# Two PSUM banks instead of one for the accumulators of a depthwise convolution, in a two-layer decoder trunk

## The chip, the cores and the metric

The kernel runs on one core of a Trainium2 chip. A core has a matrix engine (PE; PEld is its weight load, which overlaps it), a vector engine (DVE), a scalar engine (ACT), GpSimd (POOL) and a queue that issues DMAs (SP). Each engine takes its instructions in the order in which they stand in its own program, and waits on semaphores. The metric is the device time of one execution in microseconds (us).

## The reference

Two layers of a decoder block over 256 tokens of width 1024. Each layer runs a gated feed-forward block, a mixer, a second feed-forward block and a gate with an embedding. The mixer adds attention (8 heads, a window of 128, sinks) and a convolution branch. Only the mixer is touched by the change. Its convolution branch:

```python
def _conformer_conv(a, g, w_dw, b_dw, ln_g, ln_b):
    u = a * jax.nn.sigmoid(g)
    y = lax.conv_general_dilated(
        u, w_dw[:, None, :].astype(u.dtype), window_strides=(1,),
        padding=[(CONV_WIDTH - 1, 0)],
        dimension_numbers=('NWC', 'WIO', 'NWC'),
        feature_group_count=CONV_CH) + b_dw
    return jax.nn.silu(_layer_norm(y, ln_g, ln_b))
```

There are 512 channels, and each is convolved with its own 31 taps over 256 positions. The embedding that the gate needs is `e = _rms_norm(p[i] @ w_ple[i], ple_norm[i])`; its matmuls don't depend on the mixer.

## The kernel before

All matmuls are in fp32 on 128 partitions; big weights are split into a high and a low part (ACT casts, DVE or POOL subtracts), and a product takes three matmuls. PSUM has eight banks of 128x512 fp32, dealt out by three pools: `bank` (2 buffers, projections, scores and output rows), `abank` (4 buffers) and `tbank` (2 buffers, transposes). A feed-forward stage uses its four `abank` buffers as accumulators. The mixer uses the same four for the convolution, the attention output and the embedding.

The mixer writes its parts in the order of the string `ORDER = "c0 k q c1 u s0 s1 x v0 v1 p0 o0 p1 p2 o1 p3"`:

- `c0`, `c1` (`conv_half`): the two halves of the channels. A half is 256 channels, two chunks `c` of 128. Transposed inputs stand in `uT`. The first `POOL_TAPS` taps (12 in the first half, 13 in the second) are done by ACT and POOL: ACT scales a shifted input into `pp` (two instructions, one for each chunk, into one of two `pp` buffers), POOL adds it to a sum (`yp`, named `pp` in the profile). The other taps are done by DVE, one scalar_tensor_tensor for each tap and chunk, and accumulate in PSUM (`acc`); tap by tap, chunk 0 and then chunk 1. At the end DVE adds both sums into `y`.
- `k`, `q`: keys, values and queries; `s0`, `s1` (`scores`): PE makes scores, DVE masks them and takes the maximum, ACT takes exponentials of eight pieces (`sm`), DVE makes `den` and its reciprocal, POOL spreads that (`rexp`); `v0`, `v1` (`values`): PE transposes the probabilities, DVE and ACT copy them (`pT`), PE multiplies with the values into an `abank`.
- `o0`, `o1` (`attn_out`): PE transposes `rexp`, and `o` is formed from it.
- `p0` to `p3` (`emb`, which is `part` in `ple`): one quarter of the embedding each. Two matmuls (four records in the trace) into an `abank`, then ACT squares and copies it out.

Afterwards a tail is written in a fixed order (`TAIL`): output rows of attention (`a`), the layer norm of the convolution (`s` for its statistics, from `y`; `t` for the activation, from `yn`) and output rows of the convolution (`b`).

Outside of a few stretches, the order in which instructions stand on each engine is chosen when the program is built, by a scheduler with a model of its own. The convolution's instructions are written at a lower priority (`CONV_LATER = 600`). Where a tile is written twice, the build puts in waits tile by tile: for PSUM, an instruction that writes a tile waits for the last writer of that tile even where the columns differ. A new `abank` tile waits for the last reader of the tile that had its buffer.

Of the kernel before, what the change touches and what calls it, by code (L numbers as in the profile page):

```python
# [16 lines left out]
ALU = mybir.AluOpType  # L17
# [58 lines left out]
def hybrid_trunk_kernel(  # L76
# [28 lines left out]
    V, S, GP, T = nc.vector, nc.scalar, nc.gpsimd, nc.tensor  # L105
# [10 lines left out]
    def abank():  # L116
        return ps.tile([P, 512], F32, tag="acc", name="abank", bufs=4)

    def tbank():
        return pt.tile([P, 512], F32, tag="tp", name="tbank")  # L120
# [7 lines left out]
    def small(n, name="st", dt=F32):  # L128
        return wk.tile([P, n], dt, tag=f"st{n}", name=name, bufs=16 if n == 1 else 6)
# [115 lines left out]
    def gain(l, name):  # L245
        o, n = off[name]
        return pcol[:, o + l * n:o + (l + 1) * n]
# [240 lines left out]
    def mixer_stage(l, PT, EMB):  # L488
        w = w_in[l]
        X, r, r8 = [None] * 2, [None] * 2, [None] * 2  # L490
        CI, CV = [None, None], []

        def enter(t, b):
            transposed(X, t, b, gain(l, "mix"))
            if b == 1:
                r[t] = stats(t)
                r8[t] = small(1, "r8")
                GP.tensor_scalar(out=r8[t], in0=r[t], scalar1=HD ** -0.5, scalar2=None, op0=ALU.mult)

        def proj(us, t, n, hooks=()):  # L500
            b = bank()
            mms(b[:, 0:n], x_terms(X[t], us), hooks=hooks)
            return b

        def conv_load(e):
            CI[e] = unit_pair(w, 768 + e * FC, 1280 + e * FC, KD)
            CI[e].load()

        def first(hooks):
            conv_load(0)  # L510
            CV.append(proj(CI[0], 0, 512, hooks))

        def rest(nxt):
            mixer(l, w, X, r, r8, CI, CV, proj, conv_load, PT, EMB, nxt)

        return Stage(enter, first, rest)

    def mixer(l, w, X, r, r8, CI, CV, proj, conv_load, PT, EMB, nxt):
# [3 lines left out]


        cb = gain(l, "cb")
        Y = []

        def conv_half(e):
            if e == 1:
                conv_load(1)
            tb = tbank()  # L530
            for t in range(2):
                b = CV[0] if (e, t) == (0, 0) else proj(CI[e], t, 512)
                sg = wk.tile([P, FC], F32, tag="sg", name="sig", bufs=NSG)
                S.activation(sg, b[:, FC:2 * FC], AF.Sigmoid, scale=r[t])
                uu = wk.tile([P, FC], F32, tag="h1", name="u", bufs=NH1)
                V.scalar_tensor_tensor(out=uu, in0=b[:, 0:FC], scalar=r[t], in1=sg, op0=ALU.mult, op1=ALU.mult)
                for c in range(2):
                    T.transpose(tb[:, c * 256 + t * P:c * 256 + (t + 1) * P], uu[:, c * P:(c + 1) * P], ident)
            S.copy(uT[e][:, :, CW - 1:], tb.rearrange("q (c m) -> q c m", c=2))
            np_ = POOL_TAPS[e]  # L540
            acc = abank().rearrange("q (c m) -> q c m", c=2)
            with tc.high_priority(offset=-CONV_LATER):
                y = wk.tile([P, 2, 256], F32, tag="y", name="y", bufs=2)
                yp = None
                for k in range(np_):
                    pp = wk.tile([P, 2, 256], F32, tag="yp" if k == 0 else "pp", name="pp", bufs=1 if k == 0 else NPP)
                    for c in range(2):
                        ch = slice(2 * e + c, 2 * e + c + 1)
                        if k == 0:
                            S.activation(pp[:, c, :], uT[e][:, c, k:k + 256], AF.Identity,  # L550
                                         scale=wconv[l][:, ch, k], bias=cb[:, ch])
                        else:
                            S.activation(pp[:, c, :], uT[e][:, c, k:k + 256], AF.Copy, scale=wconv[l][:, ch, k])  # L553
                    if k == 0:
                        yp = pp
                    else:
                        GP.tensor_tensor(out=yp, in0=yp, in1=pp, op=ALU.add)  # L557
                for k in range(np_, CW):
                    for c in range(2):
                        ws = wconv[l][:, 2 * e + c, k:k + 1]  # L560
                        src = uT[e][:, c, k:k + 256]
                        if k == np_:
                            V.tensor_scalar(out=acc[:, c, :], in0=src, scalar1=ws, scalar2=None, op0=ALU.mult)
                        else:
                            V.scalar_tensor_tensor(out=acc[:, c, :], in0=src, scalar=ws, in1=acc[:, c, :],  # L565
                                                   op0=ALU.mult, op1=ALU.add)
                V.tensor_tensor(out=y, in0=acc, in1=yp, op=ALU.add)
            Y.append(y)


# [119 lines left out]
        for it in ORDER.split():  # L690
            if it[0] == "c":
                conv_half(int(it[1]))
            elif it == "k":
                keys_values()
            elif it == "q":
                queries()
            elif it == "u":
                up.load()
            elif it[0] == "p":
                emb(int(it[1]) // 2, int(it[1]) % 2)  # L700
            elif it[0] == "s":
                scores(int(it[1]))
            elif it == "x":
                preload(AF.Silu, DEN[0][:, 0:1])
            elif it[0] == "v":
                values(int(it[1]))
            elif it[0] == "o":
                attn_out(int(it[1]))
# [24 lines left out]
        def ln_stats(t):  # L733
            tb = tbank()
            for c in range(4):
                T.transpose(tb[:, c * P:(c + 1) * P], Y[c // 2][:, c % 2, t * P:(t + 1) * P], ident)
            bs = small(6, "bs")
# [225 lines left out]
```

## Time and profile before

| | |
|---|---|
| median of 3 runs | 1030.03 us (1029.8 to 1030.08) |
| the profiled execution | 1030.14 us, of which the trace's span is 1028.4 us |
| PE busy | 1000.8 us (97%) |
| DVE, ACT, POOL busy | 648.1, 560.4 and 168.5 us |
| mean granted TensorE clock | 0.992 of full speed |

All times inside the program are counted from the start of the span. The mixer's attention part lies at about 242 to 285 us in layer 0 and at 746 to 789 us in layer 1. PE is close to fully busy in all but the first slice and these two stretches, so time that is lost or won on PE there moves the end.

### The profile page before, as it was taken

To read this page: it belongs to the slowest core of one execution; us is meant where nothing else is said; L and a number is where in the kernel's file an instruction comes from. 1 tells how busy PE (TensorE), PEld (TensorE's weight loads), DVE (VectorE), ACT (ScalarE), POOL (GpSimd) and SP (SyncE) were. 2 spreads that over 40 slices of the span, in tenths; PEclk is the share of its full clock that TensorE was granted. 3 is DMA by queue.
4 is the path that set the end of the run, shared out by engine and by line. 5 is a ranking of instruction groups with operands and counts; after the bars stand their busy time and mean duration, and the time that the engine had idled before them with its cause. 6 is when DMAs were issued, how large, how long until landed. Compare 5 with 4: busy or idle time off the path is not lost.

```text
span 1028.4 us, 13368 instructions
## 1 busy us (share of the span) xinstructions
PE 1000.8 (97%) x4534; PEld 799.3 (78%) x4534; DVE 648.1 (63%) x1100; ACT 560.4 (54%) x1044; POOL 168.5 (16%) x210
## 2 busy tenths in 40 slices
PE   7999999998999999999999999999979999999996
PEld 5888888885568888888888888888835888888886
DVE  6764545789877455555775555457997855555553
ACT  6554444577764444545564445456787545444442
POOL 4400000147623000000000000002765500000001
PEclk9999999999999999999999999999989999999999
DMA  8965656554046655656556565655621566565621
GB/s 270 273 211 164 205 169 207 181 180 130 21 142 194 196 182 187 199 170 204 164 170 206 172 212 169 208 169 174 166 81 61 164 205 200 169 205 166 209 97 41
DMA packets 133396, 177.22 MB, mean 172 GB/s; under 512 B 9184, under 2 KB 109872, under 8 KB 133328
## 3 DMA queue, kind: packets, MB, share of 16 engines
q1 hardware_dynamic: 132144, 174.11, 53.6%
q0 software_dynamic: 1184, 2.27, 0.9%
q8 instruction: 35, 0.57, 0.2%
q14 instruction: 33, 0.27, 0.1%
HBM read 175.29 MB, written 1.05 MB: 171 GB/s over the span
## 4 chain that ended last, share of the span: by engine, by line
PE 92%; DVE 4%; ACT 2%; DMA 1%; POOL 1%; issue 1%; SPq 0%; POOLq 0%; DVEq 0%; ACTq 0%
PE bank L210 61%; PE abank L210 26%; PE tbank L351 2%; PE tbank L305 1%; DMA raw<-in_ffn_w_gate_up_dram 1%; DVE lo L132 1%; ACT sm L643 1%; DVE sm L630 1%; PE tbank L661 0%; PE tbank L482 0%; ACT hi L167 0%; POOL ms_eps L285 0%; DVE pT L665 0%; DVE xl L132 0%; DVE xg L310 0%
## 5 line engine op out<-in xcount | busy, mean ns | idle before, releaser
L132 DVE TENSOR_TENSOR lo<-raw,hi 128x512 fp32r<-128x512 f32 (+1 forms) x519 | 387.0, 791 | 175.0 <-ACT hi L167 168.5
L167 ACT CAST hi<-raw 128x512 fp32r<-128x512 f32 (+1 forms) x544 | 348.1, 689 | 209.7 <-PE abank L210 120.5
L210 PE MATMUL bank<-hi,xh 128*128 128x512 f32 (+1 forms) x904 | 353.1, 391 | 1.4 <-ACT hi L167 1.1
L210 PE MATMUL bank<-hi,xl 128*128 128x512 f32 (+1 forms) x904 | 348.6, 386 | 1.5 <-DVE xl L132 1.5
L210 PE MATMUL bank<-lo,xh 128*128 128x512 f32 (+1 forms) x904 | 348.7, 386 | 0.2
L210 PEld LDWEIGHTS bank<-hi,xl 128*128 128x128 f32 x904 | 170.2, 188 | 37.1 <-DVE xl L132 3.8
L210 PEld LDWEIGHTS bank<-hi,xh 128*128 128x128 f32 x904 | 170.4, 188 | 33.7 <-ACT hi L167 1.5
L210 PEld LDWEIGHTS bank<-lo,xh 128*128 128x128 f32 x904 | 170.5, 189 | 33.3 <-POOL lo L132 0.7
L210 PE MATMUL abank<-hi,hT_hi 128*128 128x512 f32 x352 | 137.7, 391 | 0.0
L210 PE MATMUL abank<-lo,hT_hi 128*128 128x512 f32 x352 | 137.5, 391 | 0.0
L210 PE MATMUL abank<-hi,hT_lo 128*128 128x512 f32 x352 | 137.4, 391 | 0.0
L342 ACT ACTIVATE sg<-bank,r 128x256 f32<-128x256 f32 x88 | 41.7, 474 | 158.3 <-PE bank L210 158.2
L344 DVE SCALAR_TENSOR_TENSOR h<-bank,r,sg 128x256 f32<-128x256 f32 x88 | 42.3, 481 | 130.8 <-ACT sg L342 130.8
L210 PEld LDWEIGHTS abank<-hi,hT_hi 128*128 128x128 f32 x352 | 66.1, 188 | 13.5
L210 PEld LDWEIGHTS abank<-hi,hT_lo 128*128 128x128 f32 x352 | 66.1, 188 | 13.5
L210 PEld LDWEIGHTS abank<-lo,hT_hi 128*128 128x128 f32 x352 | 66.1, 188 | 13.4
L132 POOL TENSOR_TENSOR lo<-raw,hi 128x512 fp32r<-128x512 f32 x25 | 33.1, 1347 | 239.4 <-ACT hi L167 239.4
L565 DVE SCALAR_TENSOR_TENSOR abank<-uT,wconv,abank 128x256 f32<-128x256 f32 x140 | 68.1, 487 | 3.7
L557 POOL TENSOR_TENSOR pp<-pp 128x512 f32<-128x512 f32 x46 | 59.4, 1291 | 44.2 <-ACT pp L553 42.6
L285 POOL TENSOR_SCALAR ms_eps<-ms 128x1 f32<-128x1 f32 x24 | 13.3, 554 | 260.2 <-ACT scratch L292 228.7
L553 ACT ACTIVATE pp<-uT,wconv 128x256 f32<-128x256 f32 x92 | 40.1, 500 | 4.1 <-POOL pp L557 4.1
L132 DVE TENSOR_TENSOR hT_lo<-tbank,hT_hi 128x512 fp32r<-128x512 f32 x44 | 30.4, 692 | 8.2 <-ACT hT_hi L353 5.9
(169 smaller groups left out, 680.0 us busy)
## 6 DMA issues: line engine op xcount, KB each, us to landing
raw<-in_ffn_w_gate_up_dram SPq DMA_DIRECT2D x352, 256.0 KB, 3.9
raw<-in_ffn_w_down_dram SPq DMA_DIRECT2D x88, 512.0 KB, 5.4
raw<-in_w_in_dram SPq DMA_DIRECT2D x32, 256.0 KB, 3.7
raw<-in_w_ple_gate_dram SPq DMA_DIRECT2D x16, 512.0 KB, 4.2
raw<-in_w_in_dram SPq DMA_DIRECT2D x12, 512.0 KB, 4.6
raw<-in_w_out_dram SPq DMA_DIRECT2D x8, 512.0 KB, 4.9
raw<-in_w_out_dram SPq DMA_DIRECT2D x16, 256.0 KB, 5.4
raw<-in_w_ple_dram SPq DMA_DIRECT2D x4, 512.0 KB, 4.9
```

The source lines that it names most:

```text
L132: return eng.tensor_tensor(out=lo, in0=src, in1=hi.bitcast(F32), op=ALU.subtract)
L167: S.copy(hi[:, sl, :], raw[:, sl, :])
L210: T.matmul(dst, a, b, start=first and i == 0, stop=last and i == n - 1)
L285: GP.tensor_scalar(out=e, in0=ms, scalar1=EPS, scalar2=None, op0=ALU.add)
L305: T.transpose(tb[:, i * P:(i + 1) * P], h[t][:, c * P:(c + 1) * P], ident)
L342: S.activation(s, b[:, 0:FC], AF.Silu, scale=r[t])
L344: V.scalar_tensor_tensor(out=o, in0=b[:, FC:2 * FC], scalar=r[t], in1=s, op0=ALU.mult, op1=ALU.mult)
L351: T.transpose(tb[:, k * 256 + t * P:k * 256 + (t + 1) * P], H1[j, t][:, k * P:(k + 1) * P], ident)
L553: S.activation(pp[:, c, :], uT[e][:, c, k:k + 256], AF.Copy, scale=wconv[l][:, ch, k])
L557: GP.tensor_tensor(out=yp, in0=yp, in1=pp, op=ALU.add)
L565: V.scalar_tensor_tensor(out=acc[:, c, :], in0=src, scalar=ws, in1=acc[:, c, :], op0=ALU.mult, op1=ALU.add)
L630: V.tensor_tensor_reduce(out=pr[gg][:, ks], in0=sb[:, ks], in1=masks[b], scale=1.0, scalar=sinkb[l][:, hh:hh + 1], op0=ALU.add, op1=ALU.ma ...
```

## The change

The two chunks accumulate in two `abank` tiles, `ACC[0]` and `ACC[1]`. Both are taken when the first half of the channels begins, and both halves use them: the first half the columns 0 to 255 of both, the second half the columns 256 to 511. The last addition into `y` is split into one for each chunk.

```diff
         cb = gain(l, "cb")
-        Y = []
+        Y, ACC = [], []
...
             np_ = POOL_TAPS[e]
-            acc = abank().rearrange("q (c m) -> q c m", c=2)
+            if e == 0:
+                ACC.extend(abank() for _ in range(2))
+            acc = [ACC[c][:, e * 256:(e + 1) * 256] for c in range(2)]
...
                         if k == np_:
-                            V.tensor_scalar(out=acc[:, c, :], in0=src, scalar1=ws, scalar2=None, op0=ALU.mult)
+                            V.tensor_scalar(out=acc[c], in0=src, scalar1=ws, scalar2=None, op0=ALU.mult)
                         else:
-                            V.scalar_tensor_tensor(out=acc[:, c, :], in0=src, scalar=ws, in1=acc[:, c, :],
+                            V.scalar_tensor_tensor(out=acc[c], in0=src, scalar=ws, in1=acc[c],
                                                    op0=ALU.mult, op1=ALU.add)
-                V.tensor_tensor(out=y, in0=acc, in1=yp, op=ALU.add)
+                for c in range(2):
+                    V.tensor_tensor(out=y[:, c, :], in0=acc[c], in1=yp[:, c, :], op=ALU.add)
             Y.append(y)
```

In the built program every tap of the kernel before waits for the tap just before it (the same tile), and every tap of the changed kernel for the last but one (the same chunk). As many instructions stand on each engine as before, but for one more DVE instruction at the end of each half. The order is another on PE, DVE, ACT and POOL within the two mixers; SP's DMAs stand as before. Lines behind 540 have numbers two or three higher in the changed kernel (L661 is L664, L676 is L679, L553 is L555, L565 is L567).

PE, layer 0, from the last probabilities to the embedding. `pinT` marks the embedding's matmuls (a quarter is two), `pT` those of the attention values, `rexp` and `sm` are transposes. Before:

```order
L661 MATMUL tbank<-ident,sm 128x128 x12
L210 MATMUL abank<-pT,v_100 128x512
L210 MATMUL abank<-raw_2464,pinT 128x512
L210 MATMUL abank<-raw_2466,pinT 128x512
L661 MATMUL tbank<-ident,sm 128x128 x4
L210 MATMUL abank<-pT,v_100 128x512
L210 MATMUL abank<-pT,v_101 128x512
L676 MATMUL tbank<-ident,rexp 128x128 x4
L210 MATMUL abank<-raw_2464,pinT 128x512
L210 MATMUL abank<-raw_2466,pinT 128x512
L210 MATMUL abank<-pT,v_101 128x512
```

Of the change:

```order
L664 MATMUL tbank<-ident,sm 128x128 x12
L210 MATMUL abank<-pT,v_100 128x512
L664 MATMUL tbank<-ident,sm 128x128 x4
L210 MATMUL abank<-pT,v_100 128x512
L210 MATMUL abank<-pT,v_101 128x512
L679 MATMUL tbank<-ident,rexp 128x128 x4
L210 MATMUL abank<-pT,v_101 128x512
L210 MATMUL abank<-raw_2466,pinT 128x512
L210 MATMUL abank<-raw_2468,pinT 128x512
L210 MATMUL abank<-raw_2466,pinT 128x512
L210 MATMUL abank<-raw_2468,pinT 128x512
```

The quarters p0 and p1 stood ahead of the last value matmul and now stand behind it; all four quarters follow it without a break (the last two are not shown). In the built program p0's first matmul before waits for the bank of the first half's accumulator. In the change it waits for the second half's addition into `y` of chunk 0, and p1's for that of chunk 1, since they take the banks of `ACC[0]` and `ACC[1]`.

ACT, layer 0, between the exponentials of block 0 (`128x128`) and of block 1 (`128x256`). Before:

```order
L643 ACTIVATE sm,den<-sm,nm 128x128 x7
L553 ACTIVATE pp<-uT_103,wconv_104 128x256 x4
L667 COPY pT<-tbank 128x512
L643 ACTIVATE sm,den<-sm,nm 128x256
L637 ACTIVATE es<-es 128x8
L643 ACTIVATE sm,den<-sm,nm 128x256 x7
L553 ACTIVATE pp<-uT_103,wconv_104 128x256 x4
```

Of the change:

```order
L646 ACTIVATE sm,den<-sm,nm 128x128 x7
L555 ACTIVATE pp<-uT_103,wconv_104 128x256 x4
L670 COPY pT<-tbank 128x512
L555 ACTIVATE pp<-uT_103,wconv_104 128x256 x4
L646 ACTIVATE sm,den<-sm,nm 128x256
L640 ACTIVATE es<-es 128x8
L646 ACTIVATE sm,den<-sm,nm 128x256 x7
```

Four products for two of POOL's additions have moved ahead of the exponentials of block 1. In all POOL makes twelve additions for the second half; five of them now stand ahead of its first `rexp`, two ahead of its second and five behind that.

DVE, layer 0, from the exponentials of block 1 to the end of the convolution. Before:

```order
L565 SCALAR_TENSOR_TENSOR abank<-uT_103,wconv_104,abank 128x256 x7
L665 COPY pT<-tbank 128x512
L565 SCALAR_TENSOR_TENSOR abank<-uT_103,wconv_104,abank 128x256
L645 TENSOR_TENSOR den<-den,es 128x8
L565 SCALAR_TENSOR_TENSOR abank<-uT_103,wconv_104,abank 128x256
L646 RECIPROCAL den<-den 128x8
L665 COPY pT<-tbank 128x512
L565 SCALAR_TENSOR_TENSOR abank<-uT_103,wconv_104,abank 128x256 x14
L680 TENSOR_TENSOR o<-abank,rT 128x512
L565 SCALAR_TENSOR_TENSOR abank<-uT_103,wconv_104,abank 128x256 x6
```

Of the change:

```order
L567 SCALAR_TENSOR_TENSOR abank<-uT_103,wconv_104,abank 128x256 x12
L668 COPY pT<-tbank 128x512
L648 TENSOR_TENSOR den<-den,es 128x8
L567 SCALAR_TENSOR_TENSOR abank<-uT_103,wconv_104,abank 128x256 x2
L649 RECIPROCAL den<-den 128x8
L567 SCALAR_TENSOR_TENSOR abank<-uT_103,wconv_104,abank 128x256
L668 COPY pT<-tbank 128x512
L567 SCALAR_TENSOR_TENSOR abank<-uT_103,wconv_104,abank 128x256 x9
L570 TENSOR_TENSOR y<-abank,pp 128x256 x2
L683 TENSOR_TENSOR o<-abank,rT 128x512
```

The taps now end ahead of `o`, and twelve instead of seven stand ahead of the first `pT` copy.

## Rows read from the trace of the kernel before

**Rows 1.** The page, busy us of each engine over the span.
```profile
PE 1000.8 (97%) x4534; PEld 799.3 (78%) x4534; DVE 648.1 (63%) x1100; ACT 560.4 (54%) x1044; POOL 168.5 (16%) x210
```

**Rows 2.** Waits of PE over the program: total us, times, longest.
```profile
PE abank L210 <- DVE pT L665: 2.0, 2, 1.0
PE bank L210 <- DVE m L630: 2.0, 4, 0.8
PE tbank L748 <- DVE yn L743: 1.5, 2, 0.8
PE tbank L661 <- DVE pT L665: 0.6, 2, 0.3
```

**Rows 3.** Timeline of DVE, layer 0: start, us, instruction, count, [idle before].
```profile
228.17 5.73 DVE L565 SCALAR_TENSOR_TENSOR abank<-uT,wconv,abank 128x256 f32<-128x256 f32 x11
...
237.94 0.48 DVE L536 SCALAR_TENSOR_TENSOR u<-bank,r,sig 128x256 f32<-128x256 f32 x1
238.33 3.63 DVE L565 SCALAR_TENSOR_TENSOR abank<-uT,wconv,abank 128x256 f32<-128x256 f32 x7
...
242.75 0.35 DVE L630 CUSTOM_DVE_ANT_0 sm<-bank,mask,sink 128x128 f32<-128x128 f32 x1
...
260.82 0.16 DVE L645 TENSOR_TENSOR den<-den,es 128x8 f32<-128x8 f32 x1
...
274.94 0.68 DVE L567 TENSOR_TENSOR y<-abank,pp 128x512 f32<-128x512 f32 x1
```

**Rows 4.** Timeline of PE, layer 0.
```profile
242.12 0.59 PE L210 MATMUL bank<-kT,qT 128*128 128x256 f32 x2
...
263.19 2.25 PE L210 MATMUL abank<-raw,pinT 128*128 128x512 f32 x4
...
267.87 1.88 PE L210 MATMUL abank<-raw,pinT 128*128 128x512 f32 x4
269.59 1.02 PE L210 MATMUL abank<-pT,v 128*128 128x512 f32 x2
...
284.67 0.63 PE L748 MATMUL tbank<-ident,yn 128*128 128x128 f32 x4 [0.76 <-DVE yn L743]
```

**Rows 5.** Timeline of ACT, layer 0.
```profile
252.26 1.69 ACT L553 ACTIVATE pp<-uT,wconv 128x256 f32<-128x256 f32 x4
254.16 0.59 ACT L667 COPY pT<-tbank 128x512 f32<-128x512 f32 x1 [0.21 <-PE tbank L661]
255.75 0.51 ACT L643 ACTIVATE sm<-sm,nm 128x256 f32<-128x256 f32 x1 [1.00 <-DVE es L636]
...
259.81 1.69 ACT L553 ACTIVATE pp<-uT,wconv 128x256 f32<-128x256 f32 x4
...
261.98 1.28 ACT L277 ACT_TABLE_LOAD   x1
```

**Rows 6.** Timeline of POOL, layer 0.
```profile
262.07 0.61 POOL L648 COPY rexp<-den 128x512 f32<-128x512 f32 x1
...
271.66 2.63 POOL L557 TENSOR_TENSOR pp<-pp 128x512 f32<-128x512 f32 x2
```

**Rows 7.** Timelines of ACT, DVE and PE, layer 1, one row each.
```profile
757.34 0.57 ACT L667 COPY pT<-tbank 128x512 f32<-128x512 f32 x1
...
763.86 1.16 DVE L645 TENSOR_TENSOR den<-den,es 128x8 f32<-128x8 f32 x1
...
773.68 1.02 PE L210 MATMUL abank<-pT,v 128*128 128x512 f32 x2
```

**Rows 8.** Windows: us, busy (count) of PE, PEld, DVE, ACT, POOL; PEclk, DMA share, GB/s.
```profile
246.00:250.00 4.00, 2.07 (x6) 0.67 (x5) 4.00 (x14) 3.97 (x12) 3.92 (x4) 1.00 0.62 180
250.00:254.00 4.00, 4.00 (x11) 1.89 (x9) 2.69 (x11) 3.95 (x17) 1.45 (x2) 0.57 0.28 98
...
750.00:754.00 4.00, 2.08 (x6) 0.81 (x6) 4.00 (x12) 3.97 (x13) 3.92 (x4) 1.00 0.70 215
754.00:758.00 4.00, 3.06 (x12) 1.38 (x11) 4.00 (x15) 3.91 (x15) 1.45 (x2) 1.00 0.14 49
```

## The prediction

> **What bounds the kernel now.** The page comes first: PE is busy for 1000.8 of 1028.4 us, and every other engine far less [rows 1]. So a saving on another engine counts only where PE waits for that engine, and a new wait of PE counts in full. The waits of PE come next. Those that DVE ends are few: 2.0 us for `pT`, 2.0 for `m`, 1.5 for `yn` and 0.6 for `pT` again, 6.1 us over both layers [rows 2]. All lie in the attention part of the two mixers, so the timelines of that part are what remains to be read, engine by engine, for layer 0 [rows 3 to 6] and where layer 1 differs [rows 7]. In the projections ahead of it PE runs on without a gap, and the first half of the convolution lies under them.
>
> **Taps.** A run of 11 taps takes 5.73 us and one of 7 takes 3.63 us, 0.52 us from one start to the next [rows 3]. Each of these waits for the tap just before it to end. The instruction `u`, of the same kind and shape, is followed after 0.39 us (237.94 to 238.33) by a tap that needs nothing of it [rows 3]. With two banks a tap waits for the last but one, 0.78 us back, which has ended by then; so I expect 0.39 us. Bounds: 0.52 (nothing gained) and 0.39. I take 0.39, since `u` is of the same form. For the 148 taps of both layers (140 and 8 first ones) that is 148 x 0.13 = 19 us of DVE time, not of PE time.
>
> The Trainium skill ("VectorE: DVE Perf Modes", section "The DRAIN you can't avoid") says that a vector instruction doesn't start until the pipe of the one before is empty, and that a semaphore between them costs nothing extra. By that rule the taps would gain nothing. The step from 0.52 to 0.39 us in this trace speaks against it.
>
> What the first half's shorter taps (38 of them, 38 x 0.13 = 5 us) give: PE's first score matmul starts at 242.12 and ends at 242.71, and DVE takes it up at 242.75 already [rows 3, 4]. So the attention part begins where it did, and these 5 us end as idle time of DVE. The split of the last addition costs DVE about 0.1 us in each half (two of 0.39 for one of 0.68), hidden at that place.
>
> **The bank that p0 waits for.** This is the step that decides. Before, p0 starts at 263.19 and p1 at 267.87, between the value matmuls, in time in which PE had little else [rows 4]; the convolution's second half ended only at 274.94 with `y` [rows 3], and nothing on PE waited there for it. Now p0 and p1 take the banks of `ACC`, free only after the second half's `y`, and all four quarters stand behind the last value matmul. PE takes instructions in order, so behind p0 everything waits: the other quarters, the transposes of `rexp`, the output rows of attention, the layer norm.
>
> How late is PE then? The last value matmul starts at 269.59; a quarter takes 1.72 us (267.87 to 269.59) at full clock, a value product half of it, 0.86, so it ends at 270.45, with p0 and p1 done [rows 4]. Let S be the start of p0 in the changed kernel. At S + 3.44 PE is where it was at 270.45. The loss in layer 0 is S - 267.0. In layer 1 the last value matmul starts at 773.68 and ends at 774.54 [rows 7]; the loss is S - 771.1. The work that follows is as long as before, with p2 and p3 closed up, and the wait of 0.76 us for `yn` [rows 4] stays, because `yn` hangs on the same chain behind the statistics. Later stages run at full PE, so they give nothing back.
>
> **When the second half's `y` is ready.** It needs DVE's taps and the last of POOL's twelve additions. POOL needs the products from ACT, and five of its additions now come ahead of the exponentials of block 1. Step by step in layer 0:
>
> - ACT copies `pT` from 254.16 for 0.59 us, as before. Then four products that stood behind the exponentials come first, 1.69 us (the row of four at 252.26) [rows 5]. The exponentials of block 1 start at 254.16 + 0.59 + 1.69 = 256.44, not at 255.75.
> - Eight exponentials take 4.06 us (255.75 to 259.81) [rows 5].
> - Two products for the next addition take half of 1.69, 0.85 [rows 5].
> - POOL then has an addition, a `rexp`, and five additions. With 1.31 us each (2.63 for two) and 0.61 that is 1.31 + 0.61 + 6.55 = 8.47 us [rows 6].
> - DVE adds chunk 0 into `y`, 0.48 us as `u` [rows 3].
>
> Sum: 4.06 + 0.85 + 8.47 + 0.48 = 13.86 us, so S is at the earliest 256.44 + 13.86 = 270.3. For layer 1: 757.34 + 0.57 + 1.69 = 759.60 [rows 7], and S is 773.46. The earliest losses are 3.3 and 2.4 us.
>
> What can come on top: the exponentials of block 1 may start later, because a third score matmul now stands behind two more transposes and because `den`, which took 0.16 us once, took 1.16 us another time [rows 3, 7]; both lie ahead of the maximum on DVE. I allow 0 to 1.1 us. And inside the POOL chain the second `rexp` waits for a reciprocal behind 12 taps, a copy, `den` and two taps on DVE, and later products stand behind the table load of 1.28 us on ACT and a `pT` copy of 0.6 [rows 5]: 0 to 1.9 us. I take half of each, 1.5 us in each layer, as neither bound is nearer to any row. S becomes 271.8 and 775.0, the losses 4.8 and 3.9 us, together 8.7; the bounds are 5.7 and 11.7. DVE itself isn't last: from 257 on it has 12 + 2 + 1 + 9 = 24 taps of 0.39, two copies of 0.6 and some small ones, and could end near 268.5.
>
> **The clock.** PE now stands still for some four microseconds, from the end of the values at about 267 to S. What the granted clock does then is shown only by weaker cases: after a stretch of 4 us with 2.07 us of PE work it was at 0.57 for the next 4 us, which costs 0.43 x 4 = 1.7 us of full-speed work; after one with 2.08 us it stayed at 1.00 [rows 8]. So the price is 0 to 1.7 us in each layer, 0 to 3.4 in all. The new gap is emptier than both cases, and one of two fell; I take 1.7 us for the two layers.
>
> **Sum.** 8.7 + 1.7 = 10.4 us on the profiled execution's 1030.14 us gives 1040.5. That execution is 0.11 us over the median of the runs, so I predict **1040.4 us**, slower by 1.0%. The bounds of the unknown costs are 1030.0 + 5.7 = 1035.7 and 1030.0 + 11.7 + 3.4 = 1045.1.
>
> **Rivals.**
> *Faster: DVE was what PE waited for.* If `y` is ready when PE comes to p0, the shorter taps show: up to all of the 6.1 us of PE's waits for DVE [rows 2] could go, so 1024 at best and some 1027 with half. Its place is the start of p0, and it decides if the twelfth addition ends before about 266.5 in layer 0. For it: additions stand earlier in POOL's order, and the taps of the second half get 4.7 us shorter. Against it: the exponentials, the products and POOL's own 8.47 us add up to 270.3 without any wait. Chance 0.08.
> *No change.* The gap on PE is there, but its length is made up by waits that vanish: the transposes between the exponentials and the copies of `pT` come earlier, and p0 to p3 without a break run at full clock, where p0 took 2.25 us before against 1.72 for p1 [rows 4]. Within 2 us of 1030 this needs S about 3 us ahead of my earliest. Chance 0.06.
> *The change doesn't do what it says: taps stay at 0.52 us.* This is what the rule of the Trainium skill named above would make of it. DVE's 24 taps take 3.1 us more and end near 271.6 in place of 268.5, about when POOL ends; the reciprocal, behind 14 of them, comes 1.8 us later and holds back the second `rexp` and the additions behind it. With 1 to 2 us in each layer on top of my sum the time is 1042.5 to 1044.5. Chance 0.08.
> *My forecast*, slower through the wait of p0 for the second half's `y`: chance 0.78.
>
> **Numbers.** A measurement of this kernel can tell about 0.2%, 2.1 us, from no change. Slower: 0.78 + 0.08 = 0.86; same 0.06; faster 0.08. The range leaves out the two cases that aren't slower (0.14) and little else: 1034.5 to 1045.0, the bounds of the unknown costs with about a microsecond below, where PE's smaller waits could give something back.
>
> **What would show it.** Right: taps 0.39 us apart; DVE idle ahead of the scores; a gap on PE of some 4 us in front of the first embedding matmul in both layers, ended by DVE's `y`, and POOL's last addition just ahead of that; then four quarters in a row; the transposes of `yn` 3 to 6 us later than at 284.67. The exponentials of block 1 start at 256.4 or later. Wrong in a step: taps still 0.52 apart (the rival on the pipe); `y` long done when PE comes to p0 (POOL or ACT faster than their rows); `y` held by DVE's taps instead of POOL. The sum is also wrong if the clock falls for longer than the one stretch that I took, or if PE catches up in the output rows.

## The result, and the profile after

The changed kernel takes 1043.35 us (median; 1043.22 to 1044.54) against 1030.05 us: a ratio of 1.0132, with a 95% interval of 1.0114 to 1.0149. It is slower by 1.3%; I had said 1.0%. The profiled execution is the slowest of the four and has a span of 1042.7 us, 14.3 us more than before.

The page's busy time, to be held against [rows 1]:

```profile
PE 1008.5 (97%) x4534; PEld 801.8 (77%) x4534; DVE 641.2 (61%) x1104; ACT 561.2 (54%) x1044; POOL 168.3 (16%) x210
```

DVE lost 7 us of busy time. PE got 7.7 us more of it with the same count of matmuls, so some of them ran slower; the mean granted clock over the span fell from 0.992 to 0.985. The waits of PE (total us, times, longest), against [rows 2]:

```profile
PE tbank L664 <- ACT sm L646: 6.5, 17, 1.6
PE abank L210 <- DVE y L570: 5.5, 2, 3.0
...
PE bank L210 <- DVE m L633: 2.9, 8, 0.8
PE abank L210 <- DVE pT L668: 2.2, 2, 1.3
PE tbank L664 <- DVE pT L668: 1.4, 2, 0.7
```

The row for the probabilities `sm`, made by ACT, was this before:

```profile
PE tbank L661 <- ACT sm L643: 5.9, 14, 1.9
```

The row for `y` is new: PE waits for it once in each layer. The row for `yn` is gone. The other rows shown have grown, which I hadn't forecast. DVE in layer 0 (start, us, instruction, count, [idle before]), against [rows 3]:

```profile
230.77 6.74 DVE L567 SCALAR_TENSOR_TENSOR abank<-uT,wconv,abank 128x256 f32<-128x256 f32 x17
...
243.04 0.35 DVE L633 CUSTOM_DVE_ANT_0 sm<-bank,mask,sink 128x128 f32<-128x128 f32 x1 [3.80 <-PE bank L210]
...
274.47 0.76 DVE L570 TENSOR_TENSOR y<-abank,pp 128x256 f32<-128x256 f32 x2 [3.38 <-POOL pp L559]
```

17 taps take 6.74 us: from one start to the next it is (6.74 - 0.48) / 16 = 0.39 us, where it was 0.52. DVE then stands idle for 3.80 us ahead of the score maxima, and ends `y` only when POOL has made the last addition. PE, against [rows 4], with the same place of layer 1 behind it:

```profile
271.45 1.02 PE L210 MATMUL abank<-pT,v 128*128 128x512 f32 x2
274.95 7.13 PE L210 MATMUL abank<-raw,pinT 128*128 128x512 f32 x16 [2.47 <-DVE y L570]
...
291.82 0.63 PE L751 MATMUL tbank<-ident,yn 128*128 128x128 f32 x4
...
784.57 8.83 PE L210 MATMUL abank<-raw,pinT 128*128 128x512 f32 x16 [2.99 <-DVE y L570]
```

After the last value product PE stands before p0 until 274.95, and then all four quarters run in a row. The transposes of `yn` come at 291.82 instead of 284.67, 7.15 us later [rows 4]. In layer 1 the quarters take 8.83 in place of 7.13 us, for the same 16 matmuls. ACT and POOL, against [rows 5, 6]:

```profile
256.47 0.59 ACT L670 COPY pT<-tbank 128x512 f32<-128x512 f32 x1 [2.06 <-PE tbank L664]
256.96 1.71 ACT L555 ACTIVATE pp<-uT,wconv 128x256 f32<-128x256 f32 x4
259.33 0.51 ACT L646 ACTIVATE sm<-sm,nm 128x256 f32<-128x256 f32 x1 [0.67 <-DVE nm L637]
```

```profile
264.42 1.27 POOL L559 TENSOR_TENSOR pp<-pp 128x512 f32<-128x512 f32 x1 [3.34 <-ACT pp L555]
...
269.12 5.31 POOL L559 TENSOR_TENSOR pp<-pp 128x512 f32<-128x512 f32 x4 [0.61 <-ACT pp L555]
```

The exponentials of block 1 start at 259.33, not at 255.75 as before nor at 256.44 as in my sum: the copy of `pT` ahead of them waits 2.06 us for PE, and the first of them 0.67 us more for `nm`, the negated maximum, on DVE. POOL's last row ends at 274.43; `y` follows. This is `nm` of block 1, before and in the changed kernel, and the addition on POOL beside the latter:

```profile
255.49 0.17 DVE L634 TENSOR_SCALAR nm<-m 128x8 f32<-128x8 f32 x1
...
258.10 1.20 DVE L637 TENSOR_SCALAR nm<-m 128x8 f32<-128x8 f32 x1
...
258.01 1.27 POOL L559 TENSOR_TENSOR pp<-pp 128x512 f32<-128x512 f32 x1 [1.63 <-ACT pp L555]
```

### The profile page after: what moved, and what is told of

Same layout as the page of the kernel before. It is cut to its first block, busy times and chain, and to the rows that moved or that the text cites. A ratio compares the mean times of both kernels' runs of the same rounds, so it can differ in the third digit from the quotient of the medians.

```text
span 1042.7 us, 13373 instructions
## 1 busy us (share of the span) xinstructions
PE 1008.5 (97%) x4534; PEld 801.8 (77%) x4534; DVE 641.2 (61%) x1104; ACT 561.2 (54%) x1044; POOL 168.3 (16%) x210
## 4 chain that ended last, share of the span: by engine, by line
PE 91%; DVE 5%; DMA 1%; POOL 1%; ACT 1%; issue 1%; SPq 0%; POOLq 0%; DVEq 0%; ACTq 0%
PE bank L210 62%; PE abank L210 25%; PE tbank L351 2%; DVE abank L567 2%; DMA raw<-in_ffn_w_gate_up_dram 1%; PE tbank L305 1%; POOL pp L559 1%; DVE lo L132 1%; DVE sm L633 1%; PE tbank L482 1%; DVE nm L637 0%; ACT hi L167 0%; DVE xg L310 0%; ACT L277 0%; DVE es L639 0%
## 5 line engine op out<-in xcount | busy, mean ns | idle before, releaser
L567 DVE SCALAR_TENSOR_TENSOR abank<-uT,wconv,abank 128x256 f32<-128x256 f32 x140 | 57.4, 476 | 0.0
L555 ACT ACTIVATE pp<-uT,wconv 128x256 f32<-128x256 f32 x92 | 40.5, 499 | 5.4 <-POOL pp L559 5.3
```

The lines of the kernel that those rows point to most:

```text
L567: V.scalar_tensor_tensor(out=acc[c], in0=src, scalar=ws, in1=acc[c], op0=ALU.mult, op1=ALU.add)
```

## The experiments

Each run is compared with runs of the kernel before on the same chip. "Parts" is the time from the first score matmul to the first transpose of `yn` on PE, layer 0 and layer 1 added, from the timelines of the profiled executions; before it is 42.55 + 43.16 = 85.71 us, in the changed kernel 49.41 + 50.46 = 99.87. Those 14.16 us are nearly the whole difference of the two spans (14.3).

| run | banks | p products | us | ratio (95%) | parts, us |
|---|---|---|---|---|---|
| changed kernel | two, held | behind `y` | 1043.35 | 1.0114 to 1.0149 | 99.87 |
| e1_p_free | two, held | other pool | 1032.57 | 1.0019 to 1.0043 | 87.97 |
| e2_p_free_ctl | one | other pool | 1038.57 | 1.0079 to 1.0106 | 93.48 |
| e3_hold_alone | one, held | behind `y` | 1045.21 | 1.0145 to 1.0173 | 102.50 |
| e4_sbuf_chunk | one and SBUF | as before | 1052.33 | 1.0200 to 1.0235 | 97.28 |
| e5_p_early | two, held | ahead | 1042.51 | 1.0099 to 1.0130 | 91.30 |
| e6_pool11 | two, held | behind `y` | 1037.68 | 1.0066 to 1.0090 | 92.58 |
| e7_pool11_ctl | one | as before | 1029.83 | 0.9989 to 1.0006 | 85.03 |
| e8_p_free_pool11 | two, held | other pool | 1030.50 | 0.9997 to 1.0022 | 88.21 |
| e9_placed_two | two, held | tied | 1034.95 | 1.0036 to 1.0062 | 90.66 |
| e10_placed_one | one | tied | 1027.46 | 0.9973 to 0.9990 | 83.62 |
| e11_placed_two_11 | two, held | tied | 1034.08 | 1.0033 to 1.0061 | 88.49 |
| e12_taps_behind | two, held | tied | 1024.46 | 0.9940 to 0.9968 | 80.03 |

### Is it the bank that p0 waits for? (e1, e2, e3, e4)

**e1_p_free** and **e2_p_free_ctl**: the changed kernel and the kernel before, each with one line changed in the embedding part:

```
-            b = abank()
+            b = bank()
```

> The changed kernel, but the four p products (p0 to p3) take their banks from the pool of the score and projection banks, not from the four accumulator banks, so that they need not wait for the second half's y. Theory (the loss is p0 to p3 held back by the two banks that the convolution keeps over both halves): the 5.5 us of waits for y go, the p products run in waits that PE has in any case, and the time is 1024 to 1032 us. Rival (the loss comes from the faster taps themselves, by the changed order on VectorE and ScalarE and the lower clock of the score products): the waits for y go too, but the time stays at 1036 us or more.

> Control: the kernel before, with the same edit for the p products alone. Both theories: between 1027 and 1033 us, since no p product waited for a bank there; what it differs from the kernel before is what the edit does by itself, and the former run is to be read against it.

Measured: 1032.57 and 1038.57 us. With p0 free the wait for `y` is gone and 10.8 us of the 13.3 come back, half a microsecond outside the range of my theory. The control missed its range by 5.6 us, and this row of its PE waits says where:

```profile
PE tbank L736 <- DVE y L567: 9.1, 2, 4.6
```

In the other pool the p products are issued as soon as PE has a gap, two quarters of them ahead of the first value products (layer 0), and are spent when PE later has nothing else. `y` itself comes late as well, at 281.45 in layer 0 and not at 274.94: POOL's last addition starts only at 280.16, behind small operations that wait 1.97 us for `ms` on DVE. The transposes of `y` wait 4.6 us for it in each layer. So the same edit is worth something else on either side, and e1 alone can't say what the hold costs.

**e3_hold_alone**: the kernel before, taps as they were, but the first half's bank is read once more when the second half's `y` is there:

```
+                KEPT.append(acc)
+                if e == 1:
+                    V.tensor_tensor(out=small(1, "kept"), in0=KEPT[0][:, 0, 0:1], in1=y[:, 0, 0:1], op=ALU.add)
```

> The kernel before, with one tile for each half as it was, but the first half's bank is kept until the second half's y is there, by a read of one column (one small VectorE operation added in each layer). The taps keep their 0.52 us. Theory: p0 again has to wait for the second half's y, all four p products go behind the last product of the attention, and the time is 1036 to 1046 us with no faster taps in it. Rival (order and clock after faster taps): with the taps as they were the time stays within 1028 to 1033 us.

Measured: 1045.21 us. Its PE waits and PE's timeline, layer 0:

```profile
PE abank L210 <- DVE y L567: 12.1, 2, 6.1
```

```profile
267.27 1.02 PE L210 MATMUL abank<-pT,v 128*128 128x512 f32 x2
274.27 9.90 PE L210 MATMUL abank<-raw,pinT 128*128 128x512 f32 x16 [5.98 <-DVE y L567]
```

The hold by itself, with no tap faster, costs more than the whole change. PE is at p0 at 268.29 (267.27 + 1.02) and waits 5.98 us; the quarters take 9.90 us, as the clock has fallen (granted clock 0.50 from 274 to 278 and 0.76 in the 4 us behind that). With the taps 0.52 us apart `y` waits for DVE here, whose last tap ends at 273.43, and not for POOL, which ends at 272.47. The exponentials of block 1 start at 255.62, as early as before (255.75). That the hold is enough is shown.

**e4_sbuf_chunk**: the kernel before, one bank for each half, but the second chunk accumulates in `y`, an SBUF tile:

```
-            acc = abank().rearrange("q (c m) -> q c m", c=2)
...
+                acc = [abank()[:, 0:256], y[:, 1, :]]
```

> The kernel before, with one bank for each half as it was, but the second chunk accumulates in the second half of y, in SBUF, so that an operation again waits for the last but one, and no bank is held longer. Theory: taps at 0.36 to 0.45 us, no wait for y, 1024 to 1032 us. Rival (order and clock after faster taps): taps as fast, no wait for y, but 1036 us or more. If the taps are at 0.52 us with two tiles, the shorter step of the changed kernel came from the banks and not from which operation is waited for.

Measured: 1052.33 us, and neither theory had it. PE doesn't wait for `y`; the loss is on DVE. Two neighbouring taps of DVE beside POOL's additions, two later ones, and POOL's row:

```profile
228.91 0.48 DVE L565 SCALAR_TENSOR_TENSOR abank<-uT,wconv,abank 128x256 f32<-128x256 f32 x1
229.31 1.12 DVE L565 SCALAR_TENSOR_TENSOR y<-uT,wconv,y 128x256 f32<-128x256 f32 x1
...
241.68 0.48 DVE L565 SCALAR_TENSOR_TENSOR abank<-uT,wconv,abank 128x256 f32<-128x256 f32 x1
242.07 0.48 DVE L565 SCALAR_TENSOR_TENSOR y<-uT,wconv,y 128x256 f32<-128x256 f32 x1
```

```profile
219.93 15.84 POOL L557 TENSOR_TENSOR pp<-pp 128x512 f32<-128x512 f32 x11 [12.74 <-ACT pp L553]
```

The next tap starts 0.39 us on (241.68 to 242.07) with an accumulator in PSUM and one in SBUF: the step from 0.52 to 0.39 comes from which operation a tap waits for, not from the banks. But while POOL adds, up to 235.77, a tap whose source and accumulator both lie in SBUF takes 1.12 us (median of 10 between 219 and 236), the one with its accumulator in PSUM 0.48 throughout. The Trainium skill ("SBUF — State Buffer", section "Who interferes with whom") says that a vector instruction with two SBUF inputs contends with a GpSimd instruction that reads SBUF, and that one with at most one such input doesn't, outside the modes that use both ports. For the taps this trace agrees: 1.12 against 0.48 us.

### Is it the wait, or the cover that the p products gave? (e5)

```
-ORDER = "c0 k q c1 u s0 s1 x v0 v1 p0 o0 p1 p2 o1 p3"
+ORDER = "c0 k q c1 u s0 p0 p1 s1 p2 p3 x v0 v1 o0 o1"
```

> The changed kernel with its two banks held as they are, but p0 to p3 are issued ahead of the value products, so that they take the two other accumulator banks; they land in and ahead of the first score products. They neither wait for y nor lie in PE's waits later on. Theory A (the loss is the wait itself: PE standing before p0 until y is there): the 5.5 us of waits for y go and the time is 1028 to 1033 us. Theory B (a good part of the loss is that the p products no longer fill waits of PE that are there in any case): the waits for y go as well, but the idle time shows at other places of the attention part, and the time is 1035 to 1042 us.

Measured: 1042.51 us, theory B, half a microsecond over its range. PE in layer 0:

```profile
238.27 1.88 PE L210 MATMUL abank<-raw,pinT 128*128 128x512 f32 x4
...
246.17 0.59 PE L210 MATMUL bank<-kT,qT 128*128 128x256 f32 x2
246.60 3.60 PE L210 MATMUL abank<-raw,pinT 128*128 128x512 f32 x8
```

The banks are held as in the changed kernel, no p product waits for one, and nearly nothing is won. Half of p's work stands ahead of the first score matmul, which starts at 246.17 instead of 242.41 (so "parts" holds two quarters fewer in each layer, 6.9 us in all, and isn't to be compared with the other rows). The waits that the p products filled before are empty, and PE now waits 3.8 us for the squares of the attention output as well. So taking away the 5.5 us in the row of waits isn't enough as long as the p products don't lie in gaps that are there in any case. How much of the loss in this run is that isn't shown, since the order on DVE, found below, is in it too.

### Does POOL's chain set `y`? (e6, e7, e8)

```
-POOL_TAPS = (12, 13)
+POOL_TAPS = (12, 11)
```

> The changed kernel with two taps of the second half moved from ScalarE and POOL to VectorE (11 products and 10 additions in place of 13 and 12). Theory (POOL's chain of additions sets y, and y sets p0): POOL ends 2.6 us earlier, VectorE's taps end 1.6 us later, at 272.7 in place of 271.1, so y and with it p0 come about 1.7 us earlier in each layer: 1038.5 to 1041.5 us. Rival (y is not what sets the loss, the later attention chain is): 1042.5 to 1045 us.

> Control: the kernel before with the same two taps moved. Nothing on PE waited for y there, so both theories expect 1028.5 to 1032.5 us.

> The changed kernel with the p products in the other pool of banks and the two taps moved as well. With p0 free, y is wanted only by the transposes ahead of the layer norm; the run with p free alone had VectorE idle for 2.5 us ahead of y and PE waiting 1.6 us behind it in layer 0. Theory: y comes some 2 us earlier and the time falls from 1032.6 to 1028 to 1031.5 us. Rival (y no longer matters with p free): 1032 to 1034 us.

Measured: 1037.68, 1029.83 and 1030.50 us (the last with runs from 1027.87 to 1033.72). PE's p0 and ACT's exponentials of block 1 in e6:

```profile
271.97 7.13 PE L210 MATMUL abank<-raw,pinT 128*128 128x512 f32 x16 [1.70 <-DVE y L570]
```

```profile
258.27 0.51 ACT L646 ACTIVATE sm<-sm,nm 128x256 f32<-128x256 f32 x1 [0.50 <-DVE nm L637]
```

Two additions fewer bring 5.7 us to the changed kernel and nothing that can be told to the kernel before. So `y` does set p0 here. In the changed kernel the chain of ACT and POOL makes it; in e6 POOL ends at 270.68 and DVE's taps, which are now more, at 271.59, so that `y` follows the taps. e6 is 0.8 us below the range: p0 comes 2.98 us earlier and not 1.7, because the exponentials come 1.06 us earlier too. `nm` starts where it did (258.08 against 258.10, with 12 taps of the second half ahead of it in both), but as POOL's addition is just ending it takes 0.16 us and not 1.20, and ACT is free 0.9 us earlier. With p0 free (e8) it still gives 2.1 us on e1.

### With the p products at their old places (e9, e10, e11)

`bank()` for the p products, and p0 to p2 each tied in PE's order behind the instruction that it followed before; p3 is tied behind the last transposes of `rexp` and so stands ahead of the output rows. In core:

```
+            if b == 1:
+                AFTER[0], AFTER[2] = PE_INS[-4], PE_INS[-1]
...
+            AFTER[1 if b == 0 else 3] = tr
...
-                emb(int(it[1]) // 2, int(it[1]) % 2)
+                with tc.issue_after(AFTER[int(it[1])].ins):
+                    emb(int(it[1]) // 2, int(it[1]) % 2)
```

`PE_INS` lists the matmuls, `tr` is the last transpose of `rexp`; the tie is one of order, not a wait. e9 is this on the changed kernel, e10 on the kernel before, e11 is e9 with the two taps moved as in e6.

> The changed kernel (two banks, both held over both halves), the p products in the other pool of banks, and each of them tied behind the TensorE instruction that it followed in the kernel before: p0 behind the first product of v1, p1 behind the transposes of rexp, p2 behind the last product of v1; p3 stands ahead of the output rows. Theory (the loss is p0 held for y and the cover of the p products lost with it; the shorter taps do no harm): 1026 to 1031 us. Rival (part of the loss is the changed order on ScalarE and VectorE, with the exponentials of block 1 late and the clock low): 1034 to 1040 us.

> Control for the placed run: the kernel before with the same edit of the p products, one bank for each half, taps at 0.52 us. Both theories: 1028 to 1034 us, nearly the order of the kernel before; p3 now stands ahead of the output rows, where y could be waited for by up to 1 us in each layer. The difference of the two placed runs is what the shorter taps are worth with the bank no longer in the way: theory 0 to 5 us faster; rival slower.

> The placed run with two banks, and the two taps of the second half moved from ScalarE and POOL to VectorE. If y still holds PE anywhere with p free, this is 1 to 3 us faster than the placed run alone; if not, the same within 1.5 us. Theory: 1024 to 1030 us.

Measured: 1034.95, 1027.46 and 1034.08 us. Here my theory fell. No p product waits for a bank in either, p0 to p2 stand where they did, and two banks are 7.5 us slower than one (the control is even 0.5 us below its range and under the kernel before). `y` isn't the reason (e11 is within 1 us of e9). The starts of the exponentials of block 1, e9 and then e10:

```profile
258.68 0.51 ACT L648 ACTIVATE sm<-sm,nm 128x256 f32<-128x256 f32 x1 [0.68 <-DVE nm L639]
```

```profile
256.00 0.51 ACT L645 ACTIVATE sm<-sm,nm 128x256 f32<-128x256 f32 x1 [0.73 <-DVE es L638]
```

2.68 us lie between them, though e10 starts its scores 0.52 us later (242.96 against 242.44). What is late is `nm` on DVE. DVE ahead of it, e9 and then e10 (L635 and L632 are the score maxima, L569 and L567 taps):

```profile
249.84 0.87 DVE L569 SCALAR_TENSOR_TENSOR abank<-uT,wconv,abank 128x256 f32<-128x256 f32 x2
250.63 0.47 DVE L635 CUSTOM_DVE_ANT_0 sm<-bank,mask,sink 128x256 f32<-128x256 f32 x1
...
252.24 0.87 DVE L569 SCALAR_TENSOR_TENSOR abank<-uT,wconv,abank 128x256 f32<-128x256 f32 x2
253.74 0.48 DVE L635 CUSTOM_DVE_ANT_0 sm<-bank,mask,sink 128x256 f32<-128x256 f32 x1 [0.63 <-PE bank L212]
...
257.76 0.89 DVE L639 TENSOR_SCALAR nm<-m 128x8 f32<-128x8 f32 x1
```

```profile
248.96 0.48 DVE L567 SCALAR_TENSOR_TENSOR abank<-uT,wconv,abank 128x256 f32<-128x256 f32 x1
249.35 0.47 DVE L632 CUSTOM_DVE_ANT_0 sm<-bank,mask,sink 128x256 f32<-128x256 f32 x1
...
250.16 0.48 DVE L567 SCALAR_TENSOR_TENSOR abank<-uT,wconv,abank 128x256 f32<-128x256 f32 x1
250.56 0.47 DVE L632 CUSTOM_DVE_ANT_0 sm<-bank,mask,sink 128x256 f32<-128x256 f32 x1
...
255.75 0.16 DVE L636 TENSOR_SCALAR nm<-m 128x8 f32<-128x8 f32 x1
```

With one bank the next tap isn't ready while the last one runs, and the order puts score maxima between: one tap, two maxima, one tap. With two banks there is always a second tap ready, and they stand in pairs. Ahead of `nm` of block 1 there are 12 taps of the second half in place of 7 (counted in both timelines; the changed kernel has 12 and the kernel before 7). The five more are 5 x 0.39 = 2.0 us; the score matmuls, whose banks the maxima free, come later with them (253.92 against 251.88 for the last, on PE), and everything behind the exponentials. (These are not the taps that the listing of DVE's order in the section on the change shows; that listing begins behind `nm`.)

Two other causes can be bounded. `nm` itself takes 0.89 us in e9, beside an addition of POOL that runs from 257.35 for 1.27 us, and 0.16 in e10; ACT then waits 0.68 us for it. But in e11, with the same 12 taps ahead, `nm` takes 0.15 us and the exponentials start at 257.82, and e11 is only 0.87 us faster than e9. And the clock: two of e9's five runs have a mean granted clock of 0.992 over the span, as four of e10's have, and take 1033.3 us against 1028.5 to 1028.9. So 4.4 to 4.8 of the 7.5 us are there at the same mean clock.

**e12_taps_behind**: e9, and all but the first two taps of the second half tied behind `nm` of block 1:

```
+                if it[1] == "1":
+                    with tc.issue_after(NM[1].ins):
+                        REST[0]()
```

`REST` holds the call that issues the other taps and the addition into `y`, `NM` the two `nm` operations.

> The placed run with two banks, and all but the first two taps of the second half tied behind the maximum of block 1 (its last small operation, nm) on VectorE. The placed runs showed two banks 7.5 us slower than one with no wait for a bank in either, and the exponentials of block 1 start 2.7 us later with two banks in layer 0. Theory (the taps, ready in pairs with two banks, stand in pairs ahead of the score maxima on VectorE, and so hold back the exponentials and all that follows): with the taps out of that place the exponentials of block 1 start at 256 us or earlier in layer 0 and the time is 1023 to 1028 us. Rival (the cause lies elsewhere, as in the clock or in additions on POOL beside VectorE): exponentials as late as before this edit, or early ones with the time still at 1032 to 1036 us.

Measured: 1024.46 us, faster than the kernel before by 0.3 to 0.6%, and the fastest version here. DVE, ACT and PE's waits:

```profile
252.60 0.48 DVE L651 CUSTOM_DVE_ANT_0 sm<-bank,mask,sink 128x256 f32<-128x256 f32 x1
...
253.11 0.69 DVE L686 COPY pT<-tbank 128x512 f32<-128x512 f32 x1
...
253.79 0.17 DVE L655 TENSOR_SCALAR nm<-m 128x8 f32<-128x8 f32 x1
```

```profile
255.04 0.50 ACT L664 ACTIVATE sm<-sm,nm 128x256 f32<-128x256 f32 x1
```

```profile
PE bank L212 <- DVE m L651: 4.9, 8, 1.2
...
PE tbank L682 <- ACT sm L664: 2.0, 12, 0.2
```

`nm` is done two microseconds earlier than in e10, the exponentials start at 255.04, and PE's waits for the probabilities `sm` fall from 6.5 us in the changed kernel to 2.0 (those for the maxima `m` rise from 2.9 to 4.9). The theory on the order of DVE holds: the same two banks, the same hold, the same taps of 0.39 us, 10.5 us less than e9. Part of these may be the clock. Windows of e9 and e12 (us, busy and count of PE, PEld, DVE, ACT, POOL; PEclk, DMA share, GB/s):

```profile
262.00:266.00 4.00, 3.25 (x9) 1.85 (x10) 4.00 (x10) 2.89 (x9) 1.27 (x1) 0.50 0.00 0
266.00:270.00 4.00, 4.00 (x11) 1.90 (x10) 4.00 (x11) 2.73 (x5) 3.11 (x3) 0.68 0.00 0
```

```profile
262.00:266.00 4.00, 4.00 (x17) 2.16 (x16) 4.00 (x12) 3.99 (x9) 3.24 (x4) 1.00 0.00 0
266.00:270.00 4.00, 3.97 (x10) 1.47 (x8) 3.36 (x9) 3.75 (x10) 3.41 (x4) 1.00 0.00 0
```

In e9 the granted clock is at 0.50 (the 1.2 GHz level) and 0.68 there, after a stretch in which PE went from one short wait to the next; in e12 it stays at 1.00 (in layer 1 two windows of e12 have 0.78 and 0.79). No run holds the clock still while the order changes. Nor does a run have this tie with one bank, so how much of the 1024.46 us is owed to the shorter step isn't shown.

## Why the prediction came out as it did

**Taps.** Right: 0.39 us, not 0.52. The 19 us of DVE time were too many; its busy time fell by 6.9. A tap with another operation behind it took 0.39 us of DVE's time before the change as well (248.13 to 248.52 in layer 0), and small operations took longer beside POOL: the four `nm` of the program 3.8 us in all, where it was 0.8. The rule of the Trainium skill ("VectorE: DVE Perf Modes", section "The DRAIN you can't avoid"), that a semaphore between two operations costs nothing extra (measured there on copies), isn't what this trace shows for taps: the wait for the operation just before costs 0.13 us with 256 columns. That this lies in the wait and not in the banks is shown by e4. The same section of the Trainium skill also says "A next op that is not held starts earlier"; the prediction left that out, and the 0.39 us agree with it.

**Start of the attention part.** Right: DVE idles for 3.80 us ahead of the maxima; the first score matmul starts 0.29 us later than before.

**The bank that p0 waits for.** Right in place and order: p0 stands behind the last value product, PE waits for DVE's `y`, DVE for POOL, and four quarters follow in a row. e3 shows that the hold is enough. The gap is shorter than the forecast four microseconds, 2.47 us in layer 0 and 2.99 in layer 1: the value products ended at 272.47 in layer 0 (271.45 + 1.02), not at about 267. The exponentials were late, and the time that p0 and p1 had filled between the value products didn't fall away with them. e5 adds that taking the wait away wins nearly nothing while that cover is lost.

**When `y` is ready.** This is the step that was mis-sized. I had S, the start of p0, at 270.3 at the earliest and 271.8 with the allowance; it was 274.95. The ladder's steps held: the exponentials take 4.05 us (259.33 to 263.38, against 4.06), and POOL's row from 264.42 to 274.43 is 10.01 us against 8.47 with 0 to 1.9 allowed. Its first rung didn't: the start of the exponentials of block 1 is 259.33 against 256.44, 2.89 us late where I had allowed 0 to 1.1. 2.9 + 1.5 + 0.2 us for small steps make up the 4.65 us between 270.3 and 274.95. The transposes of `yn` came 7.15 us late, where 3 to 6 was to be the sign of being right. In layer 1 S was 784.57, or 777.4 with the 7.15 us taken off that layer 0 had lost; I had 775.0. The reason is the one that e9, e10 and e12 show: I followed the changed order on ACT and POOL, and on DVE counted only the shorter taps, not that five more of them now stand ahead of the maximum. The listing of DVE's order that I went by begins behind that place. The prediction did name the small operations ahead of the maximum: the last 0.67 of the 2.89 us are `nm` itself, which takes 1.20 us beside POOL's addition; at 0.17 it would have ended before ACT was free.

**The wait for `yn`.** Wrong, and in favour of the change: 0.76 us in each layer were to stay, and the row is gone from the list of waits. With S - 267.0 = 7.95 less 0.76 layer 0 loses 7.19 us; the trace has 7.15.

**The clock.** 1.7 us for the two layers together: right, as it came, and in part by luck, as it is the middle between nothing and the full price. Layer 1's quarters take 8.83 (granted clock 0.60 from 786 to 790) against 7.13 us in layer 0. That the clock would also be lower among the score products I didn't have: 0.66 from 254 to 258, where it was 1.00.

**The rivals.** Neither "faster" nor "no change": `y` came 2.5 us after PE was ready for p0, not before. "Taps stay at 0.52" gave nearly the measured time with a mechanism that the taps refute, a reminder that the time alone doesn't settle a cause. The rival "no change" also compared unlike numbers: p0's 2.25 us is the length of its row and p1's 1.72 a step from start to start; from start to start p0 took 2.09 (263.19 to 265.28).

**The range.** That it held is in part luck. The time is 1.7 us below its upper end, the exponentials went past their allowance, and the wait for `yn`, 1.5 us over both layers, went the other way. The order of the taps on DVE ahead of `nm` wasn't in the sum.

**Two causes that don't add.** From before to e9 the two attention parts lose 4.95 us with no p product waiting for a bank: that is the order on DVE, with what the clock and the slower `nm` add to it. From e9 to the changed kernel they lose 9.21 more: the hold. But with the taps at 0.52 us the hold alone loses 16.79 (e3), and among kernels with free p products two banks are better in one arrangement (e1 against e2, 6.0 us) and worse in another (e10 against e9, 7.5 us). At the same mean clock 4.4 to 4.8 us of the difference between e9 and e10 remain; how the rest divides between the order and the clock stays open.

## What to carry to other kernels

When a buffer is held longer, look for who takes the next one from that pool, what stands behind it on its engine, and which gaps it used to fill; the loss can be larger than the wait that the profile then lists (here 9.2 us of the parts against 5.5 in the list, and 16.8 against 12.1 in e3). Work in the background that becomes ready more often also moves forward in the order of its engine: count how many of its instructions now stand ahead of each small operation that others wait for, and tie them behind it. Here the shorter step cost 13.3 us as it came, and with both put right the kernel takes 1024.46 us, some 5 us less than the kernel before; whether the tie alone, without the shorter step, would give that wasn't tried.

## What the runs showed of the hardware

A vector operation with two inputs in SBUF went from 0.48 to 1.12 us beside POOL's additions (e4, medians of 10 and 8 operations, up to 1.52 us), far more than the 0.13 us that the shorter step wins. A small operation with one input from SBUF was slower there too: `nm`, eight columns, takes 0.17 us in e12 at 253.79 with POOL idle, and 1.20 us in the changed kernel at 258.10, where POOL adds from 258.01 to 259.28. And for the same work in another order the granted clock in the attention part differed: 1.00 throughout in e12, down to 0.50 in e9 (windows of 4 us, layer 0).
